# Layer 1's MLP in a two-layer encoder: eight partial sums of the right half kept apart in HBM and combined in the last block, and re-read activation sums fetched four parts ahead

## The chip, the core and the metric

The kernel runs on one core of a Trainium2 chip. The metric is the device time of one execution in microseconds (us); less is better. A core has five engines with a program each: PE (matmul; its weight loads are shown as PEld), DVE (VectorE), ACT (ScalarE), POOL (GpSimd) and SP (SyncE). DMAs are issued by an engine into a queue; the large weight loads come from SP's, all accumulating DMAs of this kernel (destination += source) from POOL's.

## What is computed

Two encoder layers over 256 tokens of width 2048, in float32. Each layer has attention and then an MLP with a hidden width of 8192; both are modulated by six vectors made from a conditioning vector `c` (`sh`, `sc`, and the gate `g`). The change touches only the MLP of the second layer (index 1):

```python
h = _rmsnorm(x) * (1.0 + sc_m) + sh_m
y = jnp.square(jax.nn.relu(h @ w_mlp_in[l])) @ w_mlp_out[l]
x = x + g_m * y
...
return _rmsnorm(x, final_norm_g)
```

## The kernel before, in words

**Arithmetic.** Every float32 factor is split into two parts, `hi` (ACT, L158) and `lo = value - hi` (DVE, L161), and a product is three matmuls: hi·hi, hi·lo and lo·hi. So DVE makes a `lo` of every weight tile before PE can use it. Weights arrive as `raw` tiles (L177, SP's queue, 7 buffers).

**Tiling of the MLP.** The hidden width is cut into four blocks of 2048 (`fb` 0 to 3, `block_by_seven`, L1122). In a block, a loop over `m` in steps of two makes two hidden column groups: a `ps` product in PSUM (L224 and L227), joined into SBUF by ACT (L1503) and DVE (L1504), then relu and square, split into `hidh` and `hidl`. For the product with the output weights the kernel uses a scheme of seven products in place of eight (`seven`, L1323). It needs sums of activations (`mixed`, L1306: comb at L1314 to L1317, its parts `sh` and `sl`) and sums of weights (comb, L1345 to L1347). The seven products of the left half of the output columns stand in seven PSUM banks (`pp`), so that one bank of eight is left for `ps`: the next `ps` product begins only when L1504 has read the one before it. The weights of a pair go through `seven` two steps of `m` later (`pairs[-2]`).

**The right half, blocks 0 to 2** (`right_by_seven`, L1185). The hidden parts are used a second time. Four parts `q` = 0 to 3 go into four banks with plain products (`both_by_k`), four parts `q` = 4 to 7 with `seven`. The activation sums that `seven` needs for `q` = 4 to 7 are those of the left half: they were written to HBM (`stored`, L1172, tiles `mixed`) and are read back by POOL's queue (`again`, L1181, tiles `sr`): at `q` = 2, 3, 4 and 5 those of `q` = 4, 5, 6 and 7.

**Partial results.** ACT copies each PSUM bank to an SBUF tile `part` (L353), and POOL's queue writes or accumulates it into a DRAM tile `kept` (L1266 the first time, L1262 with `accum_op=add` after that). In the right half each of the eight sums is added at once to the one to four output blocks that it belongs to (`keep_product` and the table `IN_BLOCKS`): 15 DMAs a block, of 256 KB each, into four DRAM tiles. A DMA that adds to a tile waits until the one before it on that tile has landed.

**The last block** (`fb` 3). The loop over `m` is the same. At its `m` = 2 `gate(1, 5)` (L1407) lets PE transpose the gate vector `g_m` (ACT copies it, `modT`, L1413), and POOL writes it to HBM (L1414) and reads it back as a row on all partitions (L1416). The tile of that row is called `bias` in the trace. Behind the loop stands `last_right` (L1223): it reads the kept tiles (`read_kept`, L1114, tiles `acc`), adds the seven sums to them, multiplies by the row and adds to the residual `x`, for the left half in `final` (L1425, L1427), for the right half's kept tiles with `add_rows` (L1116): a multiplication on DVE (L1119) and a DMA from POOL that accumulates into the SBUF tile `x` (L1120). The last products of the right half go straight from PSUM to `final`.

**What sets the order.** A scheduler orders each engine's instructions when the program is built; at run time every engine takes its own in that order. An instruction waits on semaphores for what it reads and for the buffers that it overwrites; a DMA's semaphore rises when the DMA has landed. Most SBUF tiles named here (`part`, `sr`, `acc`, `hid`, `sh`, `sl`) come from one pool `u` of 40 tiles.

Of the kernel before, what the change touches and what calls it, by code (L numbers as in the profile page):

```python
# [13 lines left out]
ALU = mybir.AluOpType  # L14
# [5 lines left out]
NK = D // P  # L20
# [49 lines left out]
def consts():  # L70
# [28 lines left out]
RATE_M3 = 0.75  # L99
RATE_S, RATE_R, RATE_E = (0.1, 0.2), (0.8, 0.2), 0.0  # L100
RAWS = 7
IN_BLOCKS = {
    1: ((0, 2), (0, 3), (1, 2), (1, 3)), 2: ((0, 2),), 3: ((0, 3),), 4: ((1, 2),),
    5: ((0, 3), (1, 3)), 6: ((0, 3), (1, 2), (1, 3)), 7: ((1, 2), (1, 3)), 8: ((1, 3),),
}
FILL = "0|1|2|3||||rlm"


class Trunk:
# [1012 lines left out]
    def block_by_seven(self, l, fb, h, banks):  # L1122

        io = self.io
        hid, pairs, sums, stored = [], [], [None] * 7, {}
        plain = len(banks)
        end = fb == NFB - 1
        self.rate = RATE_S[l]
        for m in range(0, plain, 2):
            hid += self.relu2(self.joined(banks[m : m + 2], self.t("sum")))  # L1130
        for m in range(plain, NK, 2):
            both = self.t("sum")
            for j in range(2):
                src = io["w_m11"][NK * fb + m + j - 6] if l else io["w_m10"][NK * fb + m + j - 12]
                ps = self.wides([src], h)[0]
                self.join(ps, both[:, j])
                if len(pairs) > 1:
                    pairs[-2][j]()
            r = self.relu(both)
            parts = self.split(r, "hid")  # L1140
            hid += parts
            mixed = self.mixed(r)
            if l and not end and m >= NK // 2:
                stored[m // 2] = self.stored(mixed)
            pairs.append(self.seven(io[f"w_ms{l}"][fb, m // 2], parts, mixed, sums, m == plain, m == NK - 2))
            if end and m == 2:
                self.gate(l, 5)
        for pair in pairs[-2:]:
            for f in pair:
                f()  # L1150
        self.rate = RATE_E if end else RATE_R[l]
        if end:
            return self.last_right(hid, sums)
        light = [lambda g=g: [self.keep(i, sums[i - 1]) for i in g] for g in ((1, 2), (3, 5), (7, 6), (4,))]
        light.pop(0)()
        if l:
            return self.right_by_seven(fb, hid, plain, stored, light)
        for c in (2, 3):
            pss = [self.bank("pr") for _ in range(2)]
            for kq in range(4):  # L1160
                self.rows_by_k(pss, self.weights(io["w_m2"][l, fb, c, kq]), hid, kq)
                if light:
                    light.pop(0)()
            self.keep_right(pss, c)
# [20 lines left out]
    def right_by_seven(self, fb, hid, plain, stored, light):  # L1185

        io = self.io
        if plain:
            left = [[self.bank("pr") for _ in range(2)] for _ in range(2)]
            for m in range(0, plain, 2):  # L1190
                self.both_by_k(self.weights(io["w_ms1"][fb, m // 2]), hid, m, left, m + 2 == plain, True)
                if light:
                    light.pop(0)()
            self.keep_left(left)
        begun = [[self.bank("pr") for _ in range(2)] for _ in range(2)]
        mixed = {}
        n = NK // 4
        for q in range(n):
            if q > 1:
                mixed[n + q - 2] = self.again(stored[n + q - 2])  # L1200
            self.both_by_k(self.weights(io["w_mr"][fb, q]), hid, 2 * q, begun, q == n - 1, False)
            if light:
                light.pop(0)()
        for f in light:
            f()
        self.keep_product(8, begun[1][1])
        sums = [None, begun[0][0], begun[1][0], begun[0][1], None, None, None]
        for q in range(n, 2 * n):
            if q + 2 < 2 * n:
                mixed[q + 2] = self.again(stored[q + 2])  # L1210
            parts = hid[2 * q : 2 * q + 2]
            for f in self.seven(io["w_mr"][fb, q], parts, mixed[q], sums, q == n, q == 2 * n - 1, (2, 3, 4)):
                f()
        for i in (1, 2, 3, 5, 7, 6, 4):
            self.keep_product(i, sums[i - 1])

    def keep_product(self, i, ps):

        t = self.copy(ps, "part")
        for z in IN_BLOCKS[i]:  # L1220
            self.keep_tile(z, t)

    def last_right(self, hid, sums):  # L1223

        io = self.io
        done = self.final
        op = self.nc.vector.tensor_tensor
        acc, halves = {}, []

        def add(*group):  # L1230
            for i in group:
                op(acc[i], sums[i - 1], acc[i], ALU.add)

        def rows(c):
            for t in range(2):
                self.add_rows(acc[t, c], t, c)

        light = [
            lambda: add(3, 5), lambda: add(7, 6, 4), lambda: rows(2),
            lambda: halves.extend(self.merged(acc)), lambda: rows(3),  # L1240
            lambda: done(halves[0], 0), lambda: done(halves[1], 1),
        ]
        self.read_kept(acc, list(range(1, 9)) + [(t, c) for c in (2, 3) for t in range(2)])
        add(1, 2)
        pss = [self.bank("pr") for _ in range(2)]
        for kq in range(4):
            self.rows_by_k(pss, self.weights(io["w_m2"][1, NFB - 1, 2, kq]), hid, kq)
            light.pop(0)()
        for f in light:
            f()  # L1250
        done(pss, 2)
        done(self.rows(io["w_m2"][1, NFB - 1], hid, 3, True), 3)
# [546 lines left out]
```

## Time and profile before

| what | value |
|---|---|
| median of 3 runs | 2141.4 us (2139.91 to 2142.53) |
| profiled execution: its own time, and its span from first to last instruction | 2141.52 us, 2139.6 us |
| PE busy | 2107.5 us (98%) |
| DVE busy | 1854.9 us (87%) |
| ACT busy | 1287.6 us (60%) |
| POOL busy | 136.1 us (6%) |
| HBM read, written | 602.25 MB, 35.68 MB |
| `kept<-part` DMAs | 100 of 256 KB, median 9.2 us from issue to landing |
| `sr<-mixed` DMAs | 24 of 256 KB, median 10.0 us |

The layer's MLP runs from about 1445 us to the end of the span. Its last block begins on PE at about 1959 us and its loop over `m` ends at about 2087 us. The busy share of an engine is a mean over the whole span; what a change in one place is worth is read from the rows of that place. In a row of a timeline the columns are start, duration, engine, line, operation, tiles, and in brackets the idle time of the engine before it and what ended it.

### The profile page before, as it was taken

The numbers are of one execution on the slowest core, as the hardware profiler recorded it, in microseconds if no ns is written. First come the engines' busy times: TensorE is split into PE (matmuls) and PEld (weight loads), VectorE is DVE, ScalarE is ACT, GpSimd is POOL, SyncE is SP. The second block draws the span as 40 slices with busy tenths as digits, with TensorE's granted clock in tenths as the row PEclk, the third lists the DMA queues.
The fourth block names the chain that finished last, engine by engine and source line by source line (L and its number), as shares of the span: only waits on it lengthen the run. The fifth ranks groups of instructions, "written<-read, shape, count | busy, mean of one in ns | idle before, by whom it ended". The sixth has DMA issues, their size and how long they took to land.

```text
span 2139.6 us, 30063 instructions
## 1 busy us (share of the span) xinstructions
PE 2107.5 (98%) x11327; PEld 1821.2 (85%) x11327; DVE 1854.9 (87%) x2515; ACT 1287.6 (60%) x1904; POOL 136.1 (6%) x202
## 2 busy tenths in 40 slices
PE   7999999999999999999999999999999999999998
PEld 6899888898888888888889998888888888888886
DVE  8889888989799888879978897889988997898898
ACT  6555663564466566646454576647667666676674
POOL 0000000000000100111000000000022022012110
PEclk9999999999999999999999999999999999999999
DMA  9999898789965965899978877877689699679864
GB/s 396 423 386 341 320 352 352 283 316 405 383 218 189 372 226 211 296 404 381 388 261 319 305 288 282 298 302 266 225 309 324 223 302 285 224 228 311 252 228 148
DMA packets 110674, 643.04 MB, mean 301 GB/s; under 512 B 12800, under 2 KB 13248, under 8 KB 43712
## 3 DMA queue, kind: packets, MB, share of 16 engines
q1 hardware_dynamic: 85536, 586.41, 72.0%
q0 software_dynamic: 24272, 53.52, 10.2%
q8 instruction: 88, 1.44, 0.3%
q10 hardware_dynamic: 720, 1.19, 0.2%
q14 instruction: 58, 0.48, 0.1%
HBM read 602.25 MB, written 35.68 MB: 298 GB/s over the span
## 4 chain that ended last, share of the span: by engine, by line
PE 89%; DVE 4%; DMA 4%; issue 2%; ACT 1%; POOL 0%; SPq 0%; ACTq 0%; DVEq 0%; POOLq 0%
PE ps L224 19%; PE ps L227 10%; PE pr L318 7%; PE pr L321 7%; PE pr L319 7%; PE pp L1336 3%; PE pp L1337 3%; PE pp L1335 3%; PE pk L267 3%; DMA ada<-in_w_ada 2%; PE pk L201 2%; PE pk L205 2%; PE pk L204 2%; DVE lo L161 2%; PE pk L291 2%
## 5 line engine op out<-in xcount | busy, mean ns | idle before, releaser
L158 ACT ACTIVATE hi<-raw 128x1024 fp32r<-128x1024 f32 (+2 forms) x714 | 707.1, 1003 | 469.5 <-PE pr L319 127.2
L161 DVE TENSOR_TENSOR lo<-raw,hi 128x1024 fp32r<-128x1024 f32 (+2 forms) x714 | 807.7, 1150 | 175.7 <-ACT hi L158 107.3
L387 DVE SCALAR_TENSOR_TENSOR ada<-ada,cond 128x2048 f32<-128x2048 f32 x192 | 438.3, 2285 | 13.8 <-DMA ada<-in_w_ada 12.8
L224 PE MATMUL ps<-h,hi 128*128 128x512 f32 x1856 | 442.1, 391 | 0.9 <-DVE sum L1504 0.4
L224 PEld LDWEIGHTS ps<-h,hi 128*128 128x128 f32 x1856 | 343.8, 188 | 77.5 <-DVE sum L1504 6.7
L227 PEld LDWEIGHTS ps<-h,lo 128*128 128x128 f32 x1856 | 236.4, 191 | 8.1
L227 PE MATMUL ps<-h,lo 128*128 128x256 f32 x1856 | 238.9, 283 | 0.0
L318 PE MATMUL pr<-hi,hidh 128*128 128x512 f32 x448 | 174.4, 389 | 0.1
L319 PE MATMUL pr<-hi,hidl 128*128 128x512 f32 x448 | 174.3, 389 | 0.0
L161 DVE TENSOR_TENSOR lo<-comb,hi 128x1024 fp32r<-128x1024 f32 x114 | 138.8, 1220 | 8.0 <-ACT hi L158 3.6
L158 ACT ACTIVATE hi<-comb 128x1024 fp32r<-128x1024 f32 x114 | 120.2, 1055 | 30.3 <-PE pp L1337 12.3
L321 PE MATMUL pr<-lo,hidh 128*128 128x512 f32 x448 | 111.4, 389 | 0.0
L318 PEld LDWEIGHTS pr<-hi,hidh 128*128 128x128 f32 x448 | 84.1, 188 | 18.0 <-ACT hi L158 0.5
L321 PEld LDWEIGHTS pr<-lo,hidh 128*128 128x128 f32 x448 | 84.0, 188 | 17.6 <-DVE lo L161 0.2
L319 PEld LDWEIGHTS pr<-hi,hidl 128*128 128x128 f32 x448 | 84.1, 188 | 17.4
L201 PE MATMUL pk<-h,hi 128*128 128x256 f32 x320 | 90.4, 285 | 0.2 <-ACT h L722 0.2
L205 PE MATMUL pk<-h,lo 128*128 128x256 f32 x320 | 90.5, 283 | 0.0
L204 PE MATMUL pk<-h,hi 128*128 128x256 f32 x320 | 90.5, 283 | 0.0
L1262 POOL DMA_DIRECT2D kept<-part x76 | 67.0, 989 | 332.0 <-ACT part L353 257.4
L1503 ACT ACTIVATE sum<-ps 128x256 f32<-128x256 f32 x110 | 41.8, 383 | 75.5 <-PE ps L227 74.3
L267 PE MATMUL pk<-hf,w 128*128 128x256 f32 x384 | 83.9, 379 | 0.0
L267 PEld LDWEIGHTS pk<-hf,w 128*128 128x128 f32 x384 | 72.6, 190 | 10.2 <-ACT hf L694 0.4
(307 smaller groups left out, 3844.3 us busy)
## 6 DMA issues: line engine op xcount, KB each, us to landing
ada<-in_w_ada SPq DMA_DIRECT2D x192, 1024.0 KB, 7.5
raw<-in_w_m SPq DMA_DIRECT2D x166, 1024.0 KB, 7.5
raw<-in_w_ms SPq DMA_DIRECT2D x48, 1024.0 KB, 6.2
raw<-in_w_o SPq DMA_DIRECT2D x32, 1024.0 KB, 7.1
kept<-part POOLq DMA_DIRECT2D x100, 256.0 KB, 9.2
raw<-in_w_mr SPq DMA_DIRECT2D x24, 1024.0 KB, 6.4
raw<-in_w_m SPq DMA_DIRECT2D x24, 768.0 KB, 5.8
raw<-in_w_dv SPq DMA_DIRECT2D x16, 1024.0 KB, 5.0
```

The source lines that it names most:

```text
L158: ins = self.nc.scalar.activation(hi, v, AF.Copy)
L161: ins = self.nc.vector.tensor_tensor(lo, v, hi.bitcast(F32), ALU.subtract)
L201: ins = mm(ps, hi, x[0], start=first, stop=False, skip_group_check=shared)
L204: mm(ps, hi, x[1], start=False, stop=False, skip_group_check=shared)
L205: self.last_mac = mm(ps, lo, x[0], start=False, stop=last, skip_group_check=shared)
L224: mm(ps.rearrange("p a b -> p (a b)"), part(w, k, 0), x[2], start=k == 0, stop=False)
L227: mm(ps[:, 0], part(w, k, 1), x[0], start=False, stop=k == nk - 1)
L267: self.nc.tensor.matmul(ps, v, whole[k], start=first, stop=last, skip_group_check=True)
L318: mm(ps, xh[:, c], part(i, 0), start=kq == 0 and i == 0, stop=False)
L319: mm(ps, xl[:, c], part(i, 0), start=False, stop=False)
L321: self.last_mm = mm(ps, xh[:, c], part(i, 1), start=False, stop=kq == 3 and i == 3)
L387: ins = nc.vector.scalar_tensor_tensor(w, w, 1.0, self.cond, ALU.mult, ALU.mult, accum_out=acc[:, i : i + 1])
```

## The change

Three edits, all for layer 1.

- **The right half's sums.** `IN_BLOCKS` and `keep_product` go. Each of the eight sums is kept in a DRAM tile of its own, `("r", 1)` to `("r", 8)`: 8 DMAs a block in place of 15.
- **The last block.** A new list of 12 steps, `right_steps`, is worked off in the loop over `m`, one at each join from `m` = 2 on. Before it, when the list is made, the eight tiles are read into `acc` tiles. The first eight steps are DMAs from POOL that add one `acc` tile to another in SBUF, in the order of `IN_ORDER`; the last four are `add_rows` of the four blocks. In `last_right` the four reads and the two steps `rows(2)` and `rows(3)` go.
- **The activation sums.** Those of the last pair stay in SBUF (`mixed` at `m` = `NK` - 2 is handed on as it is), and the others are read back at `q` = 0, 1 and 2, four parts ahead of their use.

```diff
+IN_ORDER = ((6, 1), (2, 1), (7, 6), (4, 7), (6, 5), (3, 6), (5, 7), (5, 8))
...
+        right = self.right_steps() if l and end else []
...
                 if len(pairs) > 1:
                     pairs[-2][j]()
+                if m and right:
+                    right.pop(0)()
...
-                stored[m // 2] = self.stored(mixed)
+                stored[m // 2] = mixed if m == NK - 2 else self.stored(mixed)
...
+        mixed[2 * n - 1] = stored[2 * n - 1]
         for q in range(n):
-            if q > 1:
-                mixed[n + q - 2] = self.again(stored[n + q - 2])
+            if q < n - 1:
+                mixed[n + q] = self.again(stored[n + q])
...
-            if q + 2 < 2 * n:
-                mixed[q + 2] = self.again(stored[q + 2])
...
         for i in (1, 2, 3, 5, 7, 6, 4):
-            self.keep_product(i, sums[i - 1])
+            self.keep(("r", i), sums[i - 1])
+
+    def right_steps(self):
+
+        acc = {}
+        self.read_kept(acc, [("r", i) for i in (1, 6, 2, 7, 4, 5, 3, 8)])
+        add = lambda i, j: self.nc.gpsimd.dma_start(acc["r", i], acc["r", j], accum_op=ALU.add)
+        out = {2: (0, 2), 4: (1, 2), 3: (0, 3), 5: (1, 3)}
+        return [lambda p=p: add(*p) for p in IN_ORDER] + [
+            lambda i=i, tc=tc: self.add_rows(acc["r", i], *tc) for i, tc in out.items()]
...
-            lambda: add(3, 5), lambda: add(7, 6, 4), lambda: rows(2),
-            lambda: halves.extend(self.merged(acc)), lambda: rows(3),
+            lambda: add(3, 5), lambda: add(7, 6, 4), lambda: halves.extend(self.merged(acc)),
...
-        self.read_kept(acc, list(range(1, 9)) + [(t, c) for c in (2, 3) for t in range(2)])
+        self.read_kept(acc, range(1, 9))
```

The lines behind the edits move up by three: L1119, L1120, L1161, L1504 of before are L1116, L1117, L1158, L1501 after, and L1414 and L1416 (the gate) are L1411 and L1413.

How the order of the instructions changes is shown at two places. The first is POOL's program around the last block. Before, the block's keeps end with two accumulations into the last output block, then come the gate's two DMAs, and then the reads of the left half's kept tiles:

```order
L1262 DMA kept_14970<-part_18217 128x512
L1262 DMA kept_14778<-part_18212 128x512
L1414 DMA gate_18434<-modT_18436 16x128
L1416 DMA bias<-gate_18434 128x2048
L1114 DMA acc_19434<-kept_14476 128x512
```

After, at the same place, POOL's program holds the reads of the eight sums (the last of them is the first row here), the eight additions, and only then the gate. `acc_18179`, `_18181`, `_18183`, `_18185`, `_18187`, `_18189`, `_18191` and `_18193` are the sums 1, 6, 2, 7, 4, 5, 3 and 8:

```order
L1111 DMA acc_18193<-kept_14778 128x512
L1220 DMA acc_18181<-acc_18179 128x512
L1220 DMA acc_18183<-acc_18179 128x512
L1220 DMA acc_18185<-acc_18181 128x512
L1220 DMA acc_18187<-acc_18185 128x512
L1220 DMA acc_18181<-acc_18189 128x512
L1220 DMA acc_18191<-acc_18181 128x512
L1220 DMA acc_18189<-acc_18185 128x512
L1220 DMA acc_18189<-acc_18193 128x512
L1411 DMA gate_18411<-modT_18413 16x128
L1413 DMA bias<-gate_18411 128x2048
L1117 DMA x<-acc_18183 128x512
```

The gate's two DMAs have moved behind eight reads and eight additions; the four DMAs into `x` stand right behind the gate.

The second place is DVE's program in the same block, at the end of its step `m` = 4. Before, the second half of the weights of the next `ps` product (`raw_18600`) follows the first, and two rows on the sum of the second `ps` product of `m` = 4 (`ps_18527`) is read out of PSUM:

```order
L161 TENSOR_TENSOR lo_18603<-raw_18600,hi_18602 128x1024
L161 TENSOR_TENSOR lo_18607<-raw_18600,hi_18606 128x1024
L161 TENSOR_TENSOR lo_18651<-raw_18644,hi_18650 128x512
L1504 SCALAR_TENSOR_TENSOR sum_18441<-ps_18527,sum_18441 128x256
L1345 TENSOR_TENSOR comb_18796<-raw_18794 128x1024
```

After, three of the four multiplications by the gate's row stand between those two halves; `raw_18579`, `ps_18505` and `sum_18418` are the same tiles as `raw_18600`, `ps_18527` and `sum_18441` before:

```order
L158 TENSOR_TENSOR lo_18582<-raw_18579,hi_18581 128x1024
L1116 TENSOR_TENSOR acc_18183<-acc_18183,bias 128x512
L1116 TENSOR_TENSOR acc_18187<-acc_18187,bias 128x512
L1116 TENSOR_TENSOR acc_18191<-acc_18191,bias 128x512
L158 TENSOR_TENSOR lo_18586<-raw_18579,hi_18585 128x1024
L1501 SCALAR_TENSOR_TENSOR sum_18418<-ps_18505,sum_18418 128x256
L158 TENSOR_TENSOR lo_18630<-raw_18623,hi_18629 128x512
```

The multiplications have come from behind the loop (they stood after the additions of L1232) to the end of its step `m` = 4, and each reads the tile `bias` that the gate's second DMA writes. The fourth stands at the end of step `m` = 6. Elsewhere on DVE and ACT single instructions change places with a neighbour; PE's program is the same but for one matmul that moves behind a `ps` product in the last block, and SP's is the same.

More of the change, by code (lines that the diff above doesn't have):

```diff
@@ L101 @@
 RAWS = 7
[L102 to L105, printed above, removed]
+IN_ORDER = ((6, 1), (2, 1), (7, 6), (4, 7), (6, 5), (3, 6), (5, 7), (5, 8))
 FILL = "0|1|2|3||||rlm"
@@ L1205, in right_by_seven @@
             f()
-        self.keep_product(8, begun[1][1])
+        self.keep(("r", 8), begun[1][1])
         sums = [None, begun[0][0], begun[1][0], begun[0][1], None, None, None]
         for q in range(n, 2 * n):
-            if q + 2 < 2 * n:
-                mixed[q + 2] = self.again(stored[q + 2])
             parts = hid[2 * q : 2 * q + 2]
@@ L1214, in right_by_seven @@
         for i in (1, 2, 3, 5, 7, 6, 4):
-            self.keep_product(i, sums[i - 1])
[L1217 to L1221, printed above, removed]
+            self.keep(("r", i), sums[i - 1])
[6 more added lines that the diff above has]
+            lambda i=i, tc=tc: self.add_rows(acc["r", i], *tc) for i, tc in out.items()]
     def last_right(self, hid, sums):
@@ L1232, in add @@
                 op(acc[i], sums[i - 1], acc[i], ALU.add)
-        def rows(c):
-            for t in range(2):
-                self.add_rows(acc[t, c], t, c)
         light = [
-            lambda: add(3, 5), lambda: add(7, 6, 4), lambda: rows(2),
-            lambda: halves.extend(self.merged(acc)), lambda: rows(3),
+            lambda: add(3, 5), lambda: add(7, 6, 4), lambda: halves.extend(self.merged(acc)),
             lambda: done(halves[0], 0), lambda: done(halves[1], 1),
         ]
-        self.read_kept(acc, list(range(1, 9)) + [(t, c) for c in (2, 3) for t in range(2)])
+        self.read_kept(acc, range(1, 9))
         add(1, 2)
```

## The prediction

> **What bounds the kernel now.** I read the page first, then the waits, the busy time by stretches and the timelines of layer 1's MLP.
>
> ```profile
> PE 2107.5 (98%) x11327; PEld 1821.2 (85%) x11327; DVE 1854.9 (87%) x2515; ACT 1287.6 (60%) x1904; POOL 136.1 (6%) x202
> PE 89%; DVE 4%; DMA 4%; issue 2%; ACT 1%; POOL 0%; SPq 0%; ACTq 0%; DVEq 0%; POOLq 0%
> ```
>
> PE is busy 98% of the span and has 89% of the chain that ended last. So POOL's work costs nothing in itself; a change is worth what it takes from, or adds to, PE's idle time. These are the waits of PE and of its weight loads from 1430 us on that bear on the change, and the stretches of 20 us in which they fall (columns: stretch, length, then PE busy and the number of its matmuls, the other engines, clock, DMA share, GB/s).
>
> ```profile
> PEld ps L224 <- DVE sum L1504: 4.2, 14, 0.7
> PEld pr L1337 <- DMA sr<-mixed: 4.1, 3, 1.8
> PE pr L1337 <- DMA sr<-mixed: 2.8, 3, 1.3
> ...
> 1700.00:1720.00 20.00, 18.98 (x100) 15.65 (x98) 17.77 (x25) 12.29 (x17) 1.08 (x2) 1.00 0.56 192
> 1760.00:1780.00 20.00, 18.71 (x83) 15.21 (x82) 17.39 (x18) 11.61 (x13) 2.51 (x4) 1.00 0.83 267
> 1780.00:1800.00 20.00, 18.67 (x96) 15.49 (x95) 13.93 (x14) 15.35 (x19) 7.09 (x8) 1.00 1.06 347
> 1940.00:1960.00 20.00, 19.70 (x85) 15.39 (x84) 17.05 (x17) 16.32 (x22) 6.08 (x8) 1.00 0.90 316
> ```
>
> PE waits for the re-read sums (`sr`) at the ends of blocks 1 and 2: 1.29 + 1.33 + 0.30 = 2.9 us of idle time in the last three stretches. In 1700 to 1720 it is idle 1.02 us. The first row is the tight coupling in which all else hangs: with one free PSUM bank, a `ps` product waits for DVE's reading of the one before it, 14 times, never over 0.7 us. A DVE that is late by 20 us makes PE late by 20 us.
>
> **The activation sums and the keeps, blocks 0 to 2.** Per block one pair less is written and read back (four DMAs of 256 KB less), the rest is fetched at `q` = 0 to 2, and 15 keeps become 8, so 21 keeps go in three blocks. What DVE and ACT do stays the same. All of it lies beside PE's work; on its path are only the 2.9 us, and these go: the sums that were waited for stay in SBUF. The 1.02 us of block 1 may go too, if it came from the load that 15 keeps put on the DMA engines. I take 3.6 us of gain; its bounds are 0 (the fetches now queue among the left half's keeps, which were before and after them) and 4.3.
>
> **The last block, where a wait is added.** Three multiplications by the gate's row now stand in DVE's program at the end of step `m` = 4, and the row comes from a DMA that stands behind eight reads and eight additions in POOL's. When does DVE get there, and when does the row land?
>
> ```profile
> 1993.00 1.22 DVE L161 TENSOR_TENSOR lo<-raw,hi 128x1024 fp32r<-128x1024 f32 x1
> 1995.69 1.83 DVE L161 TENSOR_TENSOR lo<-raw,hi 128x1024 fp32r<-128x1024 f32 x2 [1.47 <-PE ps L227]
> 1997.43 0.42 DVE L1504 SCALAR_TENSOR_TENSOR sum<-ps,sum 128x256 f32<-128x256 f32 x1
> ...
> 1997.99 1.34 PE L224 MATMUL ps<-h,hi 128*128 128x512 f32 x5
> ```
>
> In before's clock DVE is there at 1994.2, between the `lo` of 1993.00 and that of 1995.69. Behind the multiplications on DVE stand this second `lo` and the L1504 of 1997.43, and PE's `ps` product of 1997.99 can't begin before that L1504: PE stops at 1998.0 until DVE is through. ACT has its copies and splits further ahead, SP can go on until its seven raw buffers are full; neither helps PE.
>
> The row's way, first its beginning and its present times (ACT's last `part` copies and the gate's copy, then POOL):
>
> ```profile
> 1959.58 0.60 ACT L353 ACTIVATE part<-pr 128x512 f32<-128x512 f32 x1
> 1982.21 0.25 ACT L1413 ACTIVATE modT<-pg 16x128 f32<-16x128 f32 x1
> ...
> 1956.28 3.58 POOL L1262 DMA_DIRECT2D kept<-part  x4 [12.76 <-ACT part L353]
> 1965.89 0.88 POOL L1262 DMA_DIRECT2D kept<-part  x1 [6.03 <-DMA kept<-part]
> 1968.70 0.86 POOL L1262 DMA_DIRECT2D kept<-part  x1 [1.94 <-DMA kept<-part]
> 1972.55 0.86 POOL L1262 DMA_DIRECT2D kept<-part  x1 [2.98 <-issue]
> 1976.48 0.86 POOL L1262 DMA_DIRECT2D kept<-part  x1 [3.07 <-DMA kept<-part]
> 1980.06 0.86 POOL L1262 DMA_DIRECT2D kept<-part  x1 [2.71 <-DMA kept<-part]
> ...
> 1992.79 0.78 POOL L1414 DMA_DIRECT2D gate<-modT  x1
> 2000.73 0.57 POOL L1416 DMA_DIRECT2D bias<-gate  x1 [7.16 <-DMA gate<-modT]
> ```
>
> Now the prices from issue to landing: the four keeps of 1956.28; the reads of kept tiles (L1114); the accumulations into `x` in the quiet last stretch, in the loaded one of layer 0, and over all (L1120), which are of the same kind and size as the eight additions, SBUF to SBUF, 256 KB; the gate's two DMAs; and, last, how long a multiplication by the row takes on DVE (L1119, in ns).
>
> ```profile
> L1262 POOL DMA_DIRECT2D kept<-part x4: 882/1387/1920, 1956.3 to 1957.9; - x4
> DMA to landing us min/median/max: 9.0/12.9/17.8
> ...
> L1114 POOL DMA_DIRECT2D acc<-kept x24: 538/538/911, 940.0 to 2085.4; - x24
> DMA to landing us min/median/max: 2.9/13.4/20.4
> ...
> DMA to landing us min/median/max: 3.2/3.3/4.2
> DMA to landing us min/median/max: 4.2/8.4/15.2
> DMA to landing us min/median/max: 3.2/4.7/15.2
> ...
> L1414 POOL DMA_DIRECT2D gate<-modT x4: 520/721/1197, 301.9 to 1992.8; - x4
> DMA to landing us min/median/max: 3.3/6.2/12.1
> L1416 POOL DMA_DIRECT2D bias<-gate x4: 549/573/575, 305.8 to 2000.7; - x4
> DMA to landing us min/median/max: 7.2/9.3/10.5
> ...
> L1119 DVE TENSOR_TENSOR acc<-acc,bias x12: 681/684/686, 988.9 to 2104.3; 128x512 f32<-128x512 f32 x12
> ```
>
> Step by step, in before's clock:
>
> 1. The last sum is copied at 1960.2, and the seven keeps no longer wait for each other. The first four landed from 1956.28 + 9.0 = 1965.3 to about 1957.9 + 17.8 = 1975.7, 3.5 us apart; the rows from 1965.89 on keep that pace. Three more at half of it, since the weight loads pause for full buffers: the last at 1981 (1978 to 1987).
> 2. The second read in the queue, sum 6, waits for its keep, the sixth; so all reads but one are issued at about 1980 to 1984. They land 2.9 to 13.4 us later; I take the last at 1991.5 (1984.5 to 2000).
> 3. The first addition queues behind the reads and lands at 1993 (1987 to 2003).
> 4. Three further additions, (7,6), (6,5) and (5,7), each wait for the landing of one that stands before them. Each costs 4.7 us, and two of them also 0.9 for the issue of the one ahead: 15.9 us, to 2009 (11.7 quiet, 27 loaded).
> 5. The last addition is issued, 0.9, then the gate's write, 6.2, and its read, 7.2, as here before: the row lands at 2023. Before it landed at 2000.73 + 7.2 = 2007.9, and DVE first used it at about 2097.
> 6. DVE: three multiplications at 0.68, the `lo` at 1.2 and L1504 at 0.42: 3.7, to 2026.9.
>
> So PE stands from 1998.0 to about 2027: 29 us. With all quiet ends the row lands at 2010 and the wait is 16 us; with all loaded ends at 2049, and 55 us. I stay near the quiet prices in steps 4 and 5, since a stopped DVE frees no raw buffers and the weight loads stop with it. None of this is made up later: behind the wait PE has the same work, at 98%.
>
> By the Trainium skill, "DMA: Bandwidth & Descriptors", section "Anatomy of one DMA — SWDGE (gpsimd) path", a DMA from POOL's queue takes 2.0 us and a microsecond per 436 KB, an estimate of 2.6 us here; by that step 4 would take 9.6 us and the total be 6 us less. The trace disagrees: no accumulation into `x` landed in under 3.2 us.
>
> After so long a pause PE's clock must come back. The rows show it falling and rising: the end of the span without matmuls, and the first transposes after a pause, then 2 us later.
>
> ```profile
> 2132.00:2140.00 8.00, 0.00 (x0) 0.00 (x0) 3.06 (x6) 2.35 (x5) 0.00 (x0) 0.72 0.71 262
> ...
> 16.87 2.13 PE L471 MATMUL px<-ident,xt 128*128 128x128 f32 x9
> 18.79 1.93 PE L471 MATMUL px<-ident,xt 128*128 128x128 f32 x14
> ```
>
> The granted clock is 0.72 in the last 8 us, and the same matmul starts every (2.13 - 0.42) / 8 = 0.21 us at first, then in the mean every 0.13. PE had restarted at 15.9 and was slow until about 19: 3 us at about half speed, 1.6 us lost. I add 1.6 (0 to 3.4).
>
> The Trainium skill, "TensorE: Matmul & The Clock Gate", section "Part 1: The HAM clock gate (the "warmup" mystery)", says why: half clock after an idle window of about 3.4 us, full again after as long a busy one, an estimate of 1.7 us here. The start of this trace agrees.
>
> **The tail.** Four multiplications of 0.68 us and four reads leave the stretch from 2075 on. PE has no idle time there up to 2120, so this is worth nothing; if DVE were the limit there, 2.7 us at most.
>
> **Sum.** From the profiled execution's own 2141.5 us (the median of the runs is 2141.4): -3.6 + 29.0 + 1.6 = +27, so 2168.5 us. I say 2168.
>
> **Rivals.** *The row is there in time.* If it lands by 1994.5, the wait is nothing, and the gain is all that is left: 2141.5 - 3.6 = 2138 us, not slower. For it speaks that the gate's copy is ready at 1982.5, that a read can land in 2.9 us and an addition in 3.2. But the gate's two DMAs alone take 3.3 + 7.2 at best, so the last addition would have to be out of POOL at 1984, and the sixth keep lands about 1980 only: three more links don't fit. The decision point is a chain from the sixth keep to the last addition of under 4 us.
>
> *All of it loaded.* The DMA share was 1.02 from 1980 to 2000 before, and raw loads issued ahead of the stop can stretch reads and additions to the rows' upper ends: a wait of up to 55 us and 2141.5 - 3.6 + 55 + 1.6 = 2194.5 us. Against it: SP's buffers fill within a few loads.
>
> *The early fetch does not help.* The reads of `sr` now stand among the left half's keeps, and PE could wait for them at `q` = 4 as it did at the end. Then the 3.6 us stay: 2172 us, inside the range.
>
> **How the numbers follow.** About 0.2%, 4.3 us, is what a measurement of this kernel can tell from no change. The forecast with its bounds from 16 us of wait and all the gain (2141.5 - 4.3 + 16 = 2153) up to 2186, where I cut the loaded rival, has a chance of 0.84; the loaded end above it 0.07; the row in time, or a wait of a few us, 0.09. The last has 2138 us in its middle and reaches below 2137.1 only with more gain than I count: faster 0.03, same 0.05, the few-us part slower. Slower 0.92 in all.
>
> **What would show it.** Right: in the last block PE has one idle stretch of 16 to 45 us before a `ps` product, put down to DVE's reading of `sum`, and DVE one before L1116, ended by `bias<-gate`; the gate's DMAs start some 15 us later than before; no wait for `sr` above 0.5 us; the clock dips behind the gap. Wrong: DVE passes L1116 without waiting; the eight additions take under 8 us together; or the loss lies elsewhere, for instance with ACT waiting for tiles of the pool `u` that `acc` tiles hold longer.

## The result and the profile after

| kernel | median | runs | ratio to before, 95% interval |
|---|---|---|---|
| before | 2141.4 us (2139.91 to 2143.01) | 5 | |
| after | 2173.79 us (2173.03 to 2176.29) | 5 | 1.0151, 1.0140 to 1.0163 |

The change makes the kernel 32.4 us slower; the forecast was +27 (2168, range 2153 to 2186). The profiled execution took 2175.25 us, 33.7 more than that of before. The engines' line of its page:

```profile
PE 2111.2 (97%) x11327; PEld 1823.7 (84%) x11327; DVE 1854.2 (85%) x2515; ACT 1286.6 (59%) x1904; POOL 119.1 (5%) x181
```

The work is the same (PE is busy 3.7 us longer, in a longer span), so the loss is waiting. It lies in two places.

**The last block.** DVE's timeline there, then PE's, then POOL's:

```profile
2000.76 1.21 DVE L158 TENSOR_TENSOR lo<-raw,hi 128x1024 fp32r<-128x1024 f32 x1
2025.25 1.90 DVE L1116 TENSOR_TENSOR acc<-acc,bias 128x512 f32<-128x512 f32 x3 [23.28 <-DMA bias<-gate]
2027.06 1.22 DVE L158 TENSOR_TENSOR lo<-raw,hi 128x1024 fp32r<-128x1024 f32 x1
2028.20 0.41 DVE L1501 SCALAR_TENSOR_TENSOR sum<-ps,sum 128x256 f32<-128x256 f32 x1
```

```profile
1998.61 3.79 PE L221 MATMUL ps<-h,hi 128*128 128x512 f32 x16
...
2005.31 0.39 PE L1334 MATMUL pp<-hi,hidl 128*128 128x512 f32 x1
2028.66 6.63 PE L221 MATMUL ps<-h,hi 128*128 128x512 f32 x16 [22.97 <-DVE sum L1501]
```

```profile
1966.36 4.44 POOL L1259 DMA_DIRECT2D kept<-part  x5 [0.16 <-issue]
1972.95 0.57 POOL L1111 DMA_DIRECT2D acc<-kept  x1 [2.15 <-DMA kept<-part]
1986.59 3.81 POOL L1111 DMA_DIRECT2D acc<-kept  x7 [13.07 <-DMA kept<-part]
1990.65 0.90 POOL L1220 DMA_DIRECT2D acc<-acc  x1 [0.25 <-issue]
1993.29 0.89 POOL L1220 DMA_DIRECT2D acc<-acc  x1 [1.74 <-DMA acc<-kept]
2001.63 0.86 POOL L1220 DMA_DIRECT2D acc<-acc  x1 [7.46 <-DMA acc<-acc]
2006.54 1.75 POOL L1220 DMA_DIRECT2D acc<-acc  x2 [4.04 <-DMA acc<-acc]
2011.52 1.75 POOL L1220 DMA_DIRECT2D acc<-acc  x2 [3.23 <-DMA acc<-acc]
2016.48 0.87 POOL L1220 DMA_DIRECT2D acc<-acc  x1 [3.21 <-DMA acc<-acc]
2017.02 0.84 POOL L1411 DMA_DIRECT2D gate<-modT  x1
2020.24 0.58 POOL L1413 DMA_DIRECT2D bias<-gate  x1 [2.38 <-DMA gate<-modT]
```

Read from the effect back to its cause: PE waits 23 us for one reading of a PSUM bank (L1501); DVE comes to that only behind three multiplications, before which it sat 23.3 us for the row `bias`; and POOL issued the row's two DMAs at 2017.0 and 2020.2, behind eight additions, five of which each waited for a landing. Matmuls start 0.23 us apart, so PE could have gone on at 2005.5 and loses 23.1 us. The first 16 matmuls then take 6.63 us where 16 of the same kind took 3.79 before the stop: 2.8 us more. The stretches (length, PE to POOL, clock, DMA share, GB/s) show why: the granted clock is down. Read in smaller stretches, it falls to 0.50 about 5 us after PE stopped and stays there until 2034.5, 5.8 us after PE went on, so that about the first 13 of the 16 ran slow and the last three at full clock.

```profile
2010.00:2020.00 10.00, 0.00 (x0) 0.00 (x0) 0.00 (x0) 0.00 (x0) 3.13 (x4) 0.53 0.51 92
...
2028.66:2035.30 6.64, 6.63 (x18) 5.26 (x19) 5.48 (x10) 3.77 (x5) 0.32 (x1) 0.56 1.04 242
2035.30:2045.00 9.70, 9.70 (x55) 8.47 (x55) 7.30 (x8) 6.85 (x8) 0.86 (x1) 1.00 0.60 223
```

**Blocks 1 and 2.** Before, PE came to this `ps` product at 1998.0, so by 2005.5 it was already 7.5 us late, not 3.6 early. (0.3 of it stood there at 1444 us, before this layer's MLP.) PE's waits from 1600 to 1960 us, first before, then after:

```profile
PE pr L1337 <- DMA sr<-mixed: 2.8, 3, 1.3
PE pp L1335 <- ACT hi L158: 0.9, 1, 0.9
```

```profile
PE pp L1333 <- DVE lo L158: 3.4, 2, 2.3
PE pr L1299 <- ACT hi L155: 2.8, 2, 1.7
PE pr L1333 <- DVE lo L158: 1.5, 1, 1.5
PE pr L1301 <- DVE lo L158: 1.1, 2, 0.5
PE pp L1332 <- ACT hi L155: 0.9, 1, 0.9
```

The waits for `sr` are gone, as forecast. New ones, for the two parts of the weights (`hi`, L155, and `lo`, L158), are 8.8 us; the first row of before has gone for them, so about 6 us of the 7.5 are idle time. Most of the rest is clock, 0.91 in one stretch that had 1.00 before:

```profile
1920.00:1940.00 20.00, 17.77 (x70) 13.96 (x69) 10.32 (x12) 8.12 (x11) 6.63 (x9) 0.91 1.01 245
```

ACT's timeline at the end of block 1's left half, before and then after, says why both parts are late:

```profile
1744.44 1.06 ACT L353 ACTIVATE part<-pp 128x512 f32<-128x512 f32 x2
1745.39 2.00 ACT L158 ACTIVATE hi<-raw 128x1024 fp32r<-128x1024 f32 x2
1747.29 1.08 ACT L353 ACTIVATE part<-pp 128x512 f32<-128x512 f32 x2
```

```profile
1746.81 1.07 ACT L155 ACTIVATE hi<-raw 128x1024 fp32r<-128x1024 f32 x1 [0.32 <-PE pr L1300]
1755.18 0.60 ACT L350 ACTIVATE part<-pp 128x512 f32<-128x512 f32 x1 [7.30 <-DMA kept<-part]
1757.42 0.60 ACT L350 ACTIVATE part<-pp 128x512 f32<-128x512 f32 x1 [1.65 <-DMA kept<-part]
1757.92 1.05 ACT L155 ACTIVATE hi<-raw 128x1024 fp32r<-128x1024 f32 x1
```

A copy into a `part` tile needs nothing from the landing of a keep except a free tile of the pool `u`. Before, the copies ran on; after, the fifth waits 7.3 us until an earlier keep lands and gives its tile back, and the weight splits that stand behind it on ACT wait too, with DVE's `lo` behind them (8.0 us idle at 1759.0, put down to ACT's `hi`). ACT's waits of this kind are 21.6 us in all, 6 times, against none before. The pool was short in the kernel before too, but there only POOL stood, 10.3 us in all, 4 times, before `sr` reads until a keep landed. So the theory to test has two causes: **A1**, the gate's row queued behind the additions, with DVE waiting; **A2**, the early fetch filling the pool `u`. The main rival to A2 is that the separate keeps, not the fetch, cost time in blocks 1 and 2; the one to A1, that the additions or the gate's DMAs are slow by themselves.

### The profile page after: what moved, and what is told of

Same layout as the page of the kernel before. It is cut to its first block, busy times and chain, and to the rows that moved or that the text cites. A ratio compares the mean times of both kernels' runs of the same rounds, so it can differ in the third digit from the quotient of the medians.

```text
span 2173.5 us, 30029 instructions
## 1 busy us (share of the span) xinstructions
PE 2111.2 (97%) x11327; PEld 1823.7 (84%) x11327; DVE 1854.2 (85%) x2515; ACT 1286.6 (59%) x1904; POOL 119.1 (5%) x181
## 4 chain that ended last, share of the span: by engine, by line
PE 88%; DMA 4%; DVE 3%; issue 3%; ACT 2%; POOL 0%; SPq 0%; ACTq 0%; DVEq 0%; POOLq 0%
PE ps L221 18%; PE ps L224 10%; PE pr L315 7%; PE pr L316 7%; PE pr L318 7%; PE pk L264 3%; PE pp L1333 3%; PE pp L1334 3%; PE pp L1332 3%; PE pk L198 2%; PE pk L202 2%; PE pk L201 2%; PE pk L288 2%; PE pv L302 2%; PE pv L300 2%
## 5 line engine op out<-in xcount | busy, mean ns | idle before, releaser
L155 ACT ACTIVATE hi<-raw 128x1024 fp32r<-128x1024 f32 (+2 forms) x714 | 706.3, 1003 | 457.1 <-PE pr L316 126.8
L158 DVE TENSOR_TENSOR lo<-raw,hi 128x1024 fp32r<-128x1024 f32 (+2 forms) x714 | 807.2, 1149 | 189.2 <-ACT hi L155 120.1
L221 PE MATMUL ps<-h,hi 128*128 128x512 f32 x1856 | 444.5, 393 | 23.3 <-DVE sum L1501 23.2
L158 DVE TENSOR_TENSOR lo<-comb,hi 128x1024 fp32r<-128x1024 f32 x114 | 138.6, 1219 | 8.7 <-PE ps L224 4.9
L155 ACT ACTIVATE hi<-comb 128x1024 fp32r<-128x1024 f32 x114 | 120.2, 1055 | 35.4 <-PE pp L1334 14.4
L1508 ACT ACTIVATE relu<-sum 128x512 f32<-128x512 f32 x58 | 36.5, 630 | 65.0 <-DVE sum L1501 65.0
```

Of the source, the lines that this page charges most:

```text
L155: ins = self.nc.scalar.activation(hi, v, AF.Copy)
L158: ins = self.nc.vector.tensor_tensor(lo, v, hi.bitcast(F32), ALU.subtract)
L221: mm(ps.rearrange("p a b -> p (a b)"), part(w, k, 0), x[2], start=k == 0, stop=False)
```

## Experiments

### The early fetch alone, on the kernel before

```diff
-                stored[m // 2] = self.stored(mixed)
+                stored[m // 2] = mixed if m == NK - 2 else self.stored(mixed)
...
+        mixed[2 * n - 1] = stored[2 * n - 1]
...
-            if q > 1:
-                mixed[n + q - 2] = self.again(stored[n + q - 2])
+            if q < n - 1:
+                mixed[n + q] = self.again(stored[n + q])
...
-            if q + 2 < 2 * n:
-                mixed[q + 2] = self.again(stored[q + 2])
```

> The kernel before with the activation-sum edits alone (last pair stays in SBUF, the others are read back at q = 0, 1, 2); the right half's sums are accumulated into four blocks as before. Theory A (the early fetch takes tiles of the pool u; ACT, whose program is in order, waits at a part copy for a keep to land, its weight splits come late, and PE loses 7 to 8 us in blocks 1 and 2): about 2149 us (2146 to 2152), with ACT idle over 15 us before part copies. Theory B, as the prediction had it (the early fetch only gains, and the loss in blocks 1 and 2 comes from the eight separate keeps): about 2138 us (2136.5 to 2141.4), no wait of ACT for a keep.

Measured: 2153.16 us against 2142.04, ratio 1.0049 (1.0036 to 1.0063): +11.1, above A's range of 2146 to 2152, and far from B. ACT's waits:

```profile
ACT part L353 <- DMA kept<-part: 20.9, 6, 7.9
```

The fetch alone brings ACT's waits for tiles in full; the separate keeps aren't needed for them.

### The sums kept apart alone

The changed kernel with those edits of the fetch taken back.

> The changed kernel with the activation sums stored and fetched as before (all four pairs, at q = 2 to 5); the sums kept apart and the additions in the last block stay. Theory A: the last block's wait of 23 us and some 3 us of slow clock stay, and blocks 1 and 2 are as in the kernel before: about 2167 us (2164 to 2170). Theory B (the loss in blocks 1 and 2 comes from the separate keeps, and the fetch saved something): 2174 us or more. That the row is late in the last block only because the early fetch also moved the keeps of block 3's neighbours is a third: then the wait before the first multiplication shrinks by over 5 us and the time is under 2162.

Measured: 2165.81 us, ratio 1.0110 (1.0097 to 1.0124): +23.8. In blocks 1 and 2 ACT has no wait for a keep, and PE waits only 1.6 us for `sr`, 1.2 less than before; in the last block:

```profile
DVE acc L1116 <- DMA bias<-gate: 25.5, 1, 25.5
PE ps L221 <- DVE sum L1502: 25.2, 1, 25.2
```

So the last block's wait doesn't need the early fetch, which ends the third theory, and the separate keeps alone bring no loss to blocks 1 and 2.

### The last pair alone left in SBUF, on the kernel before

```diff
-                stored[m // 2] = self.stored(mixed)
+                stored[m // 2] = mixed if m == NK - 2 else self.stored(mixed)
...
+        mixed[2 * n - 1] = stored[2 * n - 1]
...
-            if q + 2 < 2 * n:
+            if q + 2 < 2 * n - 1:
```

> The kernel before with the last pair's activation sums left in SBUF and nothing else; the other three pairs are fetched at the old places. Theory A: two tiles of u are held through the right half instead of being written and read back, but no more than two; the 2.9 us of PE's waits for re-read sums at the ends of blocks 1 and 2 go: about 2139 us (2138 to 2141). Theory B (every tile held longer costs, since ACT's part copies wait for it): 2144 us or more, with waits of ACT for keeps.

Measured: 2143.0 us against 2142.04, ratio 1.0007 (0.9998 to 1.0016). A miss for the number that A gave: no gain. B's 2144 isn't reached either, but its waits of ACT are there. PE's waits for `sr` are gone, and two tiles more are already too many:

```profile
ACT part L353 <- DMA kept<-part: 8.5, 2, 4.5
...
PE pp L1337 <- DVE lo L161: 4.3, 2, 4.0
```

One wait took the place of the other: 4.3 us for DVE's `lo`, in the place of 2.8 for `sr`. The pool had no room even for two tiles.

### The multiplications held back

The changed kernel, with its four multiplications held behind later joins of the last block. In the source they stand at the joins of `m` = 10 and 12 already, as steps 9 to 12 of the list; it was the scheduler that had put them at the end of `m` = 4 and 6. So the first edit shown changes nothing by itself, and `behind`, which fixes the order of two instructions on DVE, does it:

```diff
-                if m and right:
+                if m and right and (len(right) > 4 or m > 8):
...
-            lambda i=i, tc=tc: self.add_rows(acc["r", i], *tc) for i, tc in out.items()]
+            lambda i=i, tc=tc: self.add_rows(acc["r", i], *tc, self.last_join) for i, tc in out.items()]
...
+        if behind is not None:
+            self.behind(ins, behind)
```

> The changed kernel with its four multiplications by the gate's row held behind the joins of m = 10 and 12 of the last block; reads, additions, and gate stand where the change put them. Theory A (DVE's wait for the row is the whole loss of the last block): about 2148 us (2145 to 2151), no idle stretch of PE over 2 us there. Theory B (the reads and additions also cost by themselves, through the DMA engines or the weight loads): 2155 us or more, with PE or DVE waiting for raw loads in the last block.

Measured: 2149.53 us, ratio 1.0035 (1.0022 to 1.0047): +7.5, so 24 us less than after. PE is busy through the whole last block, with the additions and the gate where the change put them:

```profile
1960.00:2090.00 130.00, 130.00 (x692) 111.78 (x692) 113.77 (x156) 90.72 (x122) 26.50 (x37) 1.00 0.87 277
```

A1 holds: the additions on POOL cost PE nothing; DVE standing before L1116 is the whole loss of the last block. What is left, +7.5, is the fetch (ACT's waits for keeps are 20.0 us here). The two losses add up: 23.8 + 7.5 = 31.3 of 32.4. With the 11.1 that the fetch cost on the kernel before they would be 34.9; why it costs more there isn't shown.

### The additions left out

```diff
-        return [lambda p=p: add(*p) for p in IN_ORDER] + [
+        return [
...
-                if m and right:
+                if m > 4 and right:
```

> The changed kernel without its eight additions (so the right half's blocks lack their other sums); the reads, the gate and the four multiplications stand in the same order on POOL and DVE. Theory A (the row is late because the gate stands behind the chain of additions, which took from 2001 to 2020 in the changed kernel): the gate is issued right behind the reads, the row lands some 18 us earlier, DVE's wait before the first multiplication falls from 23 us to 0 to 6, the slow clock goes: 2150 to 2156 us. Theory B (the row is late because the gate's own two DMAs or the reads are slow under the weight loads): the wait stays above 12 us and the time above 2160.

Measured: 2154.71 us, ratio 1.0056 (1.0042 to 1.0070). POOL's rows and DVE's:

```profile
1989.93 0.51 POOL L1411 DMA_DIRECT2D gate<-modT  x1
1998.74 0.55 POOL L1413 DMA_DIRECT2D bias<-gate  x1 [8.30 <-DMA gate<-modT]
```

```profile
2007.28 1.90 DVE L1116 TENSOR_TENSOR acc<-acc,bias 128x512 f32<-128x512 f32 x3 [6.02 <-DMA bias<-gate]
```

The gate goes out 27 us earlier and the wait falls from 23.3 to 6.0: the chain of additions is most of it, as A1 says. But the row lands only 18 us earlier, since the two DMAs now travel among the weight loads: 8.4 us each, where the changed kernel's took 2.9 and 4.9. A had also said that the slow clock goes, and it doesn't: after PE's stop of 5.7 us the next 16 matmuls took 6.51 us.

### The gate ahead of the reads and additions

The list `right_steps()` is made behind `gate(l, 5)` at `m` = 2 instead of before the loop.

> The changed kernel with the gate's two DMAs ahead of the reads and additions in POOL's program. The scheduler now puts one multiplication at the end of m = 4 and three at the end of m = 6. Theory A: the row is no longer late, but the additions are: DVE waits for the first addition into sum 2 at m = 4 (about 8 us) and at m = 6 for the last additions (0 to 5 us): 2156 to 2165 us, the waits put down to acc<-acc. Theory B (the loss of the last block is the gate's late row alone, the additions are through by then): no wait over 2 us, 2148 us.

Measured: 2165.58 us, ratio 1.0105 (1.0092 to 1.0119), 0.6 above the range that A gave. Waits of DVE and PE in the last block:

```profile
DVE acc L1116 <- DMA acc<-acc: 10.8, 3, 4.2
...
PE ps L221 <- DVE sum L1502: 7.0, 1, 7.0
```

With the row in time, DVE waits for the additions instead, three times, and PE for DVE, here and for another 3.8 us before products that need DVE's `lo`: the gate's place alone would not have saved the change. The chain of additions was too long for where the multiplications stand.

### Fewer tiles in `u`, on the kernel before

`pool("up", 40)` becomes `pool("up", 36)`.

> The kernel before with 36 tiles in the pool u instead of 40, and no other edit: four tiles fewer, as many as the early fetch holds more at the start of the right half. Theory A: ACT waits at part copies for keeps to land, as in the changed kernel, 10 to 25 us in all in blocks 1 and 2, and PE loses 5 to 12 us: 2146 to 2154 us. Theory B (the number of tiles of u isn't the cause; the early fetch costs through the times of its transfers): no wait of ACT for keeps in blocks 1 and 2, about 2141 us.

Measured: 2151.69 us, ratio 1.0047 (1.0033 to 1.0060): +9.6. From 1600 to 1960 us:

```profile
ACT part L353 <- DMA kept<-part: 9.4, 3, 4.3
```

The same wait appears with no edit of the fetch, so the number of tiles is enough to make it. The dose is smaller than expected (9.4 us in all, not 10 to 25 and PE's `pp` wait for DVE's `lo` there 6.3 us), and part of the loss is elsewhere: in layer 0's stretch from 480 to 960 us PE is busy 476.2 us against 479.5.

### More tiles in `u`

Four tiles more in the changed kernel, paid for with a raw buffer (`RAWS = 6`), and the kernel before with that same loss:

> The changed kernel with four more tiles in the pool u (44) and, to make room for them, six raw buffers instead of seven. Theory A (too few tiles of u): ACT no longer waits over 2 us in all at part copies for keeps in blocks 1 and 2, the gaps of PE there go, and of the 32 us about 7.5 come back: 2166 us plus what one raw buffer less costs, which the run of the kernel before with six raw buffers tells. Theory B (the loss in blocks 1 and 2 isn't one of tiles): ACT's waits and PE's gaps stay.

> The kernel before with six raw buffers, as a measure for the run with 44 tiles of u. Both theories: 2141 us plus the price of the missing buffer, 0 to 10 us.

Measured: 2179.36 us (ratio 1.0175, 1.0160 to 1.0191) and 2152.86 us (1.0050, 1.0034 to 1.0065). The buffer costs the kernel before 11.1 us; without that the changed kernel with 44 tiles would be at 2168.3, 5.5 below itself with 40. ACT's waits fall from 21.6 us to

```profile
ACT part L350 <- DMA kept<-part: 8.6, 2, 4.6
```

and PE's idle time from 1580 to 1960 us from 9.8 to 5.8 us, where the kernel before has 4.4. Most of A2's loss goes, not all. Counted from the diff, the early fetch holds four tiles more than before at `q` = 0, but six at `q` = 1 and 2. (A's limit of 2 us of waiting was missed. The 5.5 us assume that the buffer costs the same in both kernels, which isn't shown; in the last block PE's stop is longer here, 28.6 us for 23.0. The idle time of blocks 1 and 2 is the better measure.)

### Without either loss

The sums kept apart, late multiplications, the old fetch:

> The sums kept apart as in the change, the multiplications by the row held behind the joins of m = 10 and 12, the activation sums stored and fetched as before. Theory A: neither of the two losses is left; of the waits for re-read sums 1 us is gone as in the run with the sums kept apart alone: 2139 to 2141.5 us. Theory B (keeping the sums apart costs by itself in the last block or the tail): 2144 us or more.

Measured: 2140.87 us, ratio 0.9995 (0.9986 to 1.0004): as A said, no difference from before that shows. PE still waits for `sr` in block 1, and POOL's rows there show a second cause, a read that stands behind a keep that waits for PE:

```profile
1778.79 0.50 PE L1337 MATMUL pr<-hi,sr 128*128 128x512 f32 x1 [1.75 <-DMA sr<-mixed]
1785.17 0.50 PE L1337 MATMUL pr<-hi,sr 128*128 128x512 f32 x1 [1.32 <-DMA sr<-mixed]
```

```profile
1767.51 0.90 POOL L1262 DMA_DIRECT2D kept<-part  x1 [10.39 <-ACT part L350]
1768.08 1.96 POOL L1183 DMA_DIRECT2D sr<-mixed  x3
```

So the last kernel moves the reads, by one step:

```diff
+        mixed[n + 2] = self.again(stored[n + 2])
         self.keep(("r", 8), begun[1][1])
...
-            if q + 2 < 2 * n:
-                mixed[q + 2] = self.again(stored[q + 2])
+            if q == n:
+                mixed[q + 3] = self.again(stored[q + 3])
```

> The run with the sums kept apart, late multiplications and the old fetch, with one more edit: the third pair's re-read activation sums are issued ahead of the keep of sum 8 in POOL's program, and the last pair's one part earlier. In that run these reads stood behind that keep, which waits for PE, and PE waited 1.9 and 1.5 us for them in block 1. Theory A (tiles of u are short only while the left half's parts are being kept, so a fetch ten us later does no harm): these waits go, no new wait of ACT over 1 us: 2136.5 to 2139 us. Theory B (any earlier fetch makes ACT wait for tiles): 2142 us or more.

Measured: 2137.72 us against 2141.79, ratio 0.9982 (0.9974 to 0.9991), the fastest of all. No wait for `sr` and none of ACT for a keep is left; PE in block 2, 186.97 us busy before:

```profile
1770.00:1960.00 190.00, 189.73 (x955) 159.97 (x954) 163.70 (x204) 134.41 (x174) 28.23 (x38) 1.00 0.79 258
```

The 2.9 us that the prediction counted on can be had, but with a fetch at most one part earlier, not one four parts ahead of use.

## Why the prediction was right and where it was wrong

Measured in the clock of before (7.5 us off the times after), the last block followed its steps:

| step | forecast | measured |
|---|---|---|
| 1 the sixth keep, for which the second read waits | about 1980 | 1979 (read issued at 1986.6) |
| 2 reads issued | 1980 to 1984 | 1979 to 1983 |
| 3 first addition landed | 1993 | by 1994 (the third, which waits for it, issued at 2001.6) |
| 4 last link's wait ends | 2009 | 2009 (2016.5) |
| 5 row landed | 2023 | 2017.6 (2025.1) |
| 6 DVE, then PE | 3.7 | 3.4 |

- **The wait in the last block** (29.0): right in place, mechanism and releaser, and with 23.1 within its bounds of 16 and 55. Nearly the whole difference of 5.9, 5.6, is one price in step 5, the gate's write and read. I took 6.2 and 7.2 from rows of before in which the loads ran; they took 2.9 and 4.9. The reason I gave for quiet prices, that a stopped DVE stops the weight loads, held here: SP's queue issued none between 1999.7 and 2028.3, and the DMA share was 0.51 from 2010 to 2020. Where DVE doesn't stop, in the kernel with late multiplications, the same two took 8.0 and 7.6. The loaded bound was added up too low: 2003, 27, 0.9, 12.1 and 10.5 from its rows give a row at 2053.5, not 2049, and a wait of 59 us.
- **The clock** (1.6): 2.8 measured, within its bounds and right in kind. The price came from the spacing of the transposes at the start alone: the granted clock in before's stretch from 10 to 20 us reads 1.00, so that trace doesn't show that the clock made them slow. The dip behind the gap is shown in the kernel after. The Trainium skill, "TensorE: Matmul & The Clock Gate", section "Part 1: The HAM clock gate (the "warmup" mystery)", lets the first 3.4 us or so run at half clock. The trace shows more: 5.8 us at a granted clock of 0.50.
- **The step that failed** is the gain of the early fetch: "On its path are only the 2.9 us, and these go: the sums that were waited for stay in SBUF", 3.6 us of gain, with bounds of 0 and 4.3. The sums were there in time, but I priced only the transfer and not the tiles that it fills. It became a loss of 7.5, outside the bounds by 7.5, and outside the rival of the early fetch too, which had it at 0. The prediction named ACT waiting for tiles of `u` as a way to be wrong, but blamed `acc` tiles; the fetch alone, without any of those `acc` tiles, did it.
- **The sum.** 7.5 + 23.1 + 2.8 = 33.4 of the 33.7 between the profiled executions. The miss of 5.9 us in the wait and that of 11.1 in the gain pull apart, so the total is nearer than its terms: that the forecast of 2168 came within 6 us of the result is in part luck.
- **Rivals.** *All of it loaded* fell for the reason given. *The row is there in time* would have needed more than the right order on POOL: with the gate first, DVE waited for the additions.
- **The tail**, priced at nothing: 0.3 us is left over, in line with that.

## What to carry to other kernels

Before a value is fetched earlier or kept longer, count the buffers of its pool at that time: an engine that takes a buffer in program order stops, with everything behind it, until a transfer elsewhere gives one back. An instruction that needs a late DMA should not stand on a bound engine ahead of what another engine waits for; the same DMA chain cost 24 us or nothing, by the place of four short multiplications. That place was the scheduler's choice, not the source's, so look at the order it made. Take the price of a transfer from rows with the load that will be there when it travels, not from where it stood before.

## What was not expected of the hardware

- The same two small DMAs of the gate took 2.9 and 4.9 us while the weight loads stood still, 8.0 and 7.6, or 8.4 and 8.4, among them.
- After 23 us without matmuls the next 16 took 6.63 us instead of 3.79; after 5.7 us (the kernel without additions) they took 6.51, and after 7.0 us (the gate ahead) 5.91. A short pause costs the clock about as much as a long one.
